# One change to an attention kernel on one core: value products in pieces of two blocks, value scaling on GpSimd, own weight buffers for ScalarE, a new start, planner constants tuned anew

## The chip, the cores and the metric

The kernel runs on one core of one Trainium2 chip. The metric is the device time of one execution in microseconds (us), as the median of several executions. The profile is one execution; its span is some 1.9 us shorter than the device time.

PE is the matrix engine, ACT is ScalarE, DVE is VectorE, POOL is GpSimd. SP issues most of the DMAs.

## The reference, cut to what matters

```python
# q: (8, 1024, 16, 64), k and v: (8, 1024, 64); all 16 heads share k and v
scores = np.matmul(q, k.transpose(0, 1, 3, 2)) / np.sqrt(head_dim)
weights = np.exp(scores - np.max(scores, axis=-1, keepdims=True))
weights = weights / np.sum(weights, axis=-1, keepdims=True)
attn_out = np.matmul(weights, v)
```

The exponentials are the bulk: 8 x 16 x 1024 x 1024 of them. The kernel skips the maximum and gets the row sums from a column of ones beside the values.

## The kernel before

The work is cut into 64 pairs of heads, and each pair into 8 weight tiles (128 keys x 2 heads x 1024 queries), 512 tiles in all. PE makes a tile's scores in two halves ("qk"), each half in one of three PSUM slots. A tile then takes one of two ways. On ACT, two ACTIVATEs of 128x1024 do the exponential. On DVE, two evictions ("z") turn the scores into 16-bit patterns, and four more steps make three factors of them (here `wt`, `z` and `m`), each of which is multiplied with its own copy of the values, scaled by a constant. PE adds up the value products ("av") in one of two accumulators, for three groups of 6, 4 and 6 blocks of 128 queries. DVE divides the result by its sums ("rec", "norm").

A planner in Python runs once, when the kernel is built. It simulates the engines with the constants below and fixes the order of instructions on PE, ACT and DVE. So an engine that is late makes the ones behind it wait (in e6 PE stands 1.13 us for one late DVE factor).

```python
ACT_P, ACT_L = 0.905, 1.19
LAST, SPLIT = 14, 4          # the last 14 tiles all go to ACT
WBUFS = 25
ZBUFS = 6
TERMS = (1.0, 1.017578125, 0.66650390625)
BLOCKS = (0, 6, 10, 16)
# ... in plan(): a group is entered once all 8 tiles of its pair are known
                parts = [
                    (j, k) for j in range(NKT) for k in range(len(TERMS))
                    if k == 0 or NKT * p + j in vtiles
                ] if nt >= NKT * (p + 1) else None
# ...
            cost = AV_B * size[pick[0][1]] if pick else 0.0
# ... in the kernel:
    def scale_v(b):
        st = kst[b]
        st["v"] = vals[b % 2]
        for x, c in zip(st["v"], TERMS):
            nc.vector.tensor_scalar(
                out=x[:, :, 0:D], in0=st["vn"], scalar1=c, scalar2=None, op0=ALU.mult)
# ...
    def exp_act(t, c):
        nc.scalar.activation(
            out=wt[t][:, :, c * QC : (c + 1) * QC], in_=sc.pop((t, c)), func=EXP, scale=ascale
        )
# ...
    def value(p, grp, j, k, n, end, s):
        # ...
        for x in range(BLOCKS[grp], BLOCKS[grp + 1]):    # all 4 or 6 blocks of the group
            # ... one 128x128 weight load and one product of 65 columns for each block
```

Both kinds of tile take their weight buffer from one pool of 25 (`wt`), so an ACTIVATE may have to wait for the earlier user of its buffer on DVE or on ACT itself, in addition to PE. The start transposes all keys and queries of the first pair before the first score.

The softmax here doesn't subtract the row's maximum and nothing guards it: scores larger than these inputs give would overflow.

## Time and profile before

| | before |
|---|---|
| device time, median | 766.85 us (4 runs before the prediction), 766.3 us with the later ones (13 runs) |
| first ACTIVATE starts, last one ends | 8.2 us, 759.4 us |
| ACTIVATEs | 814, 0.904 us apart when nothing hinders (median of the start times) |
| lost between ACTIVATEs | 14.7 us: the sum over all of them of the distance of starts less 0.904 us |
| tail after the last ACTIVATE | 6.4 us |

Three lines from the head of the page and its group lines; after the bar come busy us and mean ns of one instruction, then idle us before them.

```profile
span 765.8 us, 29940 instructions
PE 739.3 (97%) x13616; PEld 486.6 (64%) x13616; DVE 721.0 (94%) x1043; ACT 750.4 (98%) x817; POOL 45.7 (6%) x61
...
L411 ACT ACTIVATE wt<-sc 128x1024 f16<-128x1024 f32 x814 | 748.0, 1241 | 3.8 <-PE sc L401 3.4
...
L434 DVE TENSOR_SCALAR wt<-z 128x2048 uint16<-128x2048 uint16 x105 | 71.2, 678 | 0.2
...
L319 DVE TENSOR_SCALAR vals<-vn 128x512 f16<-128x512 f32 x24 | 9.1, 432 | 0.0
```

ACT is busy for nearly the whole span. So the time is the number of ACTIVATEs times their distance, plus what comes before the first and after the last. PE's 97% says less, since matmul spans overlap: the page has 8192 value products of 194 ns each in the mean, but busy for only 377 us together. The mean of 1241 ns is not the cost of one ACTIVATE either: 814 of them would make 1010 us, and the page has them busy for 748. Successive ones overlap, and the distance of their starts (0.904 us) is what counts.

The front, from the timeline of ACT (start us, length us, what, idle before it and what ended that):

```profile
8.23 13.86 ACT L411 ACTIVATE wt<-sc 128x1024 f16<-128x1024 f32 x15 [0.67 <-PE sc L401]
22.75 1.02 ACT L411 ACTIVATE wt<-sc 128x1024 f16<-128x1024 f32 x1 [0.66 <-PE sc L401]
24.17 2.92 ACT L411 ACTIVATE wt<-sc 128x1024 f16<-128x1024 f32 x3 [0.39 <-PE sc L401]
27.79 2.91 ACT L411 ACTIVATE wt<-sc 128x1024 f16<-128x1024 f32 x3 [0.70 <-PE sc L401]
```

The stream begins at 8.23 us and breaks several times between 22 and 28 us. The timeline of DVE over the same stretch:

```profile
12.27 0.69 DVE L434 TENSOR_SCALAR wt<-z 128x2048 uint16<-128x2048 uint16 x1
12.88 0.69 DVE L437 TENSOR_SCALAR u<-z 128x2048 uint16<-128x2048 uint16 x1
...
14.74 1.22 DVE L423 TENSOR_SCALAR z<-sc 128x1024 uint16<-128x1024 f32 x1
...
18.87 1.45 DVE L319 TENSOR_SCALAR vals<-vn 128x512 f16<-128x512 f32 x3
20.24 0.68 DVE L437 TENSOR_SCALAR u<-z 128x2048 uint16<-128x2048 uint16 x1
20.84 1.21 DVE L423 TENSOR_SCALAR z<-sc 128x1024 uint16<-128x1024 f32 x1
```

The three scalings of the values stand at 18.87 us in DVE's order, ahead of the eviction at 20.84 us, whose PSUM slot PE needs for the next scores. PE's timeline has the wait (1.19 us, until an eviction "z" was done):

```profile
22.11 1.03 PE L401 MATMUL sc<-qt,k2t 64*128 64x512 f16 x4 [1.19 <-DVE z L423]
```

The end, from the timeline of all engines:

```profile
756.05 3.32 ACT L411 ACTIVATE wt<-sc 128x1024 f16<-128x1024 f32 x3
...
757.60 4.14 PE L454 MATMUL acc<-vals,wt 128*128 128x65 f16 x128
...
762.01 0.56 DVE L476 TENSOR_TENSOR osb<-acc,rec 128x384 f32<-128x384 f32 x1
```

PE has 128 value products left after its last score. ACT ends at 759.37 us (756.05 + 3.32), and PE 2.4 us after it.

Busy us of the engines in the middle (PE, PEld, DVE, ACT, POOL; then clock, DMA share, GB/s):

```profile
100.00:600.00 500.00, 491.87 (x9170) 326.04 (x9169) 485.86 (x702) 499.10 (x545) 32.39 (x34) 1.00 0.58 102
```

DVE is at 97.2% there (485.86 of 500).

### The profile page before, as it was taken

What the parts mean: (1) busy time and instruction counts of PE and PEld (TensorE: products, weight loads), DVE (VectorE), ACT (ScalarE), POOL (GpSimd) and SP (SyncE); (2) the same over time, 40 slices, a digit from 0 to 9 for tenths busy, and PEclk for the clock granted to TensorE, in tenths of its full rate; (3) what the DMA queues carried; (4) which work ended last, traced back from release to release, by engine and by line L of the source; (5) the groups of instructions that cost most, each with busy time, mean ns of one, the idle gap of its engine ahead of it and who ended that gap; (6) DMA issues with size and microseconds to landing.
All of it is one profiled execution on the core that took longest, in us unless ns stands there. A gap on an engine that the chain in (4) does not pass through costs nothing.

```text
span 765.8 us, 29940 instructions
## 1 busy us (share of the span) xinstructions
PE 739.3 (97%) x13616; PEld 486.6 (64%) x13616; DVE 721.0 (94%) x1043; ACT 750.4 (98%) x817; POOL 45.7 (6%) x61
## 2 busy tenths in 40 slices
PE   6998999999999999999999999999999999999997
PEld 2565666666666666666666666666666666666676
DVE  5999999999999999899999999999999999999982
ACT  6999999999999999999999999999999999999996
POOL 2100010000100001000010000100001000000000
PEclk9999999999999999999999999999999999999999
DMA  7955675355754447644584644756529455532323
GB/s 110 137 96 103 106 105 110 73 105 105 112 109 89 95 88 109 115 100 83 95 130 84 111 102 82 112 112 99 108 65 132 89 94 102 97 72 58 85 57 85
DMA packets 189839, 75.06 MB, mean 98 GB/s; under 512 B 90256, under 2 KB 188560, under 8 KB 189712
## 3 DMA queue, kind: packets, MB, share of 16 engines
q1 hardware_dynamic: 140544, 54.14, 32.0%
q0 software_dynamic: 47840, 18.35, 21.7%
q8 instruction: 106, 1.74, 0.9%
q10 hardware_dynamic: 1328, 0.66, 0.3%
q14 instruction: 21, 0.17, 0.1%
HBM read 39.58 MB, written 33.55 MB: 96 GB/s over the span
## 4 chain that ended last, share of the span: by engine, by line
ACT 39%; PE 35%; DVE 20%; issue 5%; DMA 0%; POOL 0%; DVEq 0%; ACTq 0%
ACT wt L411 39%; PE acc L454 20%; PE sc L401 14%; DVE z L423 7%; DVE m L441 3%; DVE m L440 3%; DVE osb L476 2%; DVE u L437 2%; DVE wt L434 1%; DVE vals L319 1%; DVE rec L467 1%; DMA kn<-in_k_dram 0%; PE qps L394 0%; POOL k L369 0%; PE kps L389 0%
## 5 line engine op out<-in xcount | busy, mean ns | idle before, releaser
L411 ACT ACTIVATE wt<-sc 128x1024 f16<-128x1024 f32 x814 | 748.0, 1241 | 3.8 <-PE sc L401 3.4
L454 PE MATMUL acc<-vals,wt 128*128 128x65 f16 x8192 | 377.2, 194 | 2.5 <-issue 1.7
L401 PE MATMUL sc<-qt,k2t 64*128 64x512 f16 x2048 | 356.8, 388 | 14.5 <-ACT wt L411 6.4
L454 PEld LDWEIGHTS <-wt 128*128 128x128 f16 x8192 | 295.4, 97 | 116.6 <-issue 116.1
L423 DVE TENSOR_SCALAR z<-sc 128x1024 uint16<-128x1024 f32 x210 | 256.1, 1220 | 21.2 <-PE sc L401 16.6
L401 PEld LDWEIGHTS <-k2t 64*128 64x128 f16 x2048 | 100.6, 93 | 100.1 <-issue 55.4
L440 DVE TENSOR_TENSOR m<-u 128x2048 f16<-128x2048 f16 x105 | 126.4, 1204 | 0.2
L441 DVE TENSOR_TENSOR m<-z,m 128x2048 f16<-128x2048 f16 x105 | 126.3, 1203 | 0.0
L454 PE MATMUL acc<-vals,z 128*128 128x65 f16 x1680 | 103.2, 194 | 0.0
L476 DVE TENSOR_TENSOR osb<-acc,rec 128x384 f32<-128x384 f32 (+1 forms) x192 | 96.6, 503 | 0.4
L454 PE MATMUL acc<-vals,m 128*128 128x65 f16 x1680 | 94.4, 194 | 0.0
L454 PEld LDWEIGHTS <-m 128*128 128x128 f16 x1680 | 67.1, 97 | 32.1 <-issue 32.1
L454 PEld LDWEIGHTS <-z 128*128 128x128 f16 x1680 | 71.0, 97 | 20.2 <-issue 20.2
L434 DVE TENSOR_SCALAR wt<-z 128x2048 uint16<-128x2048 uint16 x105 | 71.2, 678 | 0.2
L437 DVE TENSOR_SCALAR u<-z 128x2048 uint16<-128x2048 uint16 x105 | 70.9, 675 | 0.0
L343 POOL DMA_DIRECT2D qn<-in_q_dram x32 | 29.6, 926 | 616.6 <-DMA qt<-qn 615.2
L467 DVE RECIPROCAL rec<-acc 128x6 f32<-128x6 f32 (+1 forms) x192 | 34.8, 181 | 13.7 <-PE acc L454 13.7
L304 POOL DMA_DIRECT2D k<-in_k_dram x14 | 13.8, 991 | 0.0
L319 DVE TENSOR_SCALAR vals<-vn 128x512 f16<-128x512 f32 x24 | 9.1, 432 | 0.0
L389 PE MATMUL kps<-ident,k 128*128 128x128 f16 x8 | 1.2, 305 | 5.3 <-POOL k L369 5.1
L391 ACT COPY k2t<-kps 128x512 f16<-128x512 f16 x2 | 1.2, 586 | 3.3 <-PE kps L389 3.3
L385 DVE CAST k<-kn 128x512 f16<-128x512 f32 x1 | 0.4, 426 | 4.1 <-DMA kn<-in_k_dram 4.1
(16 smaller groups left out, 8.6 us busy)
## 6 DMA issues: line engine op xcount, KB each, us to landing
out_dram<-osb SPq DMA_DIRECT2D x63, 512.0 KB, 3.7
qn<-in_q_dram POOLq DMA_DIRECT2D x31, 512.0 KB, 7.9
vn<-in_v_dram SPq DMA_DIRECT2D x8, 256.0 KB, 3.1
k<-in_k_dram POOLq DMA_DIRECT2D x14, 128.0 KB, 7.2
qf<-in_q_dram ACTq DMA_DIRECT2D x2, 256.0 KB, 4.3
qt<-qn SPq DMA_TRANSPOSE x32, 4.8
out_dram<-osb SPq DMA_DIRECT2D x2, 192.0 KB, 2.6
kn<-in_k_dram SPq DMA_DIRECT2D x1, 256.0 KB, 3.4
```

The lines of the kernel that those rows point to most:

```text
L319: nc.vector.tensor_scalar(out=x[:, :, 0:D], in0=st["vn"], scalar1=c, scalar2=None, op0=ALU.mult)
L343: nc.gpsimd.dma_start(out=qn[ps[0]].rearrange("p (c r) x -> p c (r x)", r=len(ps)), in_=q[b, :, 2 * hp : 2 * hp + 2 * len(ps), :].rearrang ...
L401: nc.tensor.matmul(sc[t, c][:, h, :], kst[p // HP]["k2t"][64 * h : 64 * h + 64, j, :], qt[p][64 * h : 64 * h + 64, 4 * c : 4 * c + 4, :], ...
L411: nc.scalar.activation(out=wt[t][:, :, c * QC : (c + 1) * QC], in_=sc.pop((t, c)), func=EXP, scale=ascale)
L423: nc.vector.tensor_scalar(out=z[:, :, c * QC : (c + 1) * QC], in0=sc.pop((t, c)), scalar1=vscale, scalar2=(15 + math.log2(C0)) * ONE, op0= ...
L434: lambda: V.tensor_scalar(out=wt[t].bitcast(U16), in0=z, scalar1=0xFC00, scalar2=None, op0=ALU.bitwise_and),
L437: lambda: V.tensor_scalar(out=u, in0=z, scalar1=1023, scalar2=14 << 10, op0=ALU.bitwise_and, op1=ALU.bitwise_or),
L440: lambda: V.tensor_tensor(out=m, in0=h, in1=h, op=ALU.mult),
L441: lambda: V.tensor_tensor(out=m, in0=z.bitcast(FP16), in1=m, op=ALU.mult),
L454: nc.tensor.matmul(acc[p, grp][:, o : o + D + 1], w[:, h, i * P : (i + 1) * P], kst[p // HP]["v"][k][:, j, 0 : D + 1], start=(n == 0 and o ...
L467: nc.vector.reciprocal(out=rec[p, grp][:, 0 : a.shape[1]], in_=a[:, :, D])
L476: nc.vector.tensor_tensor(out=o.rearrange("p i (h d) -> p (i h) d", h=2)[:, BLOCKS[grp] : BLOCKS[grp + 1], :], in0=a[:, :, 0:D], in1=rec.p ...
```

## The change

Its intent is to have fewer ACTIVATEs, fewer waits between them, and shorter ends. It has five parts.

1. Value products are given out in pieces of two blocks (`STEP = 2`) instead of whole groups, and a group takes up tiles as they become known.
2. The scaling of the values moves from DVE to GpSimd. That of batch 0 also comes earlier, right after the first two entries of the plan.
3. ACT's tiles get 26 weight buffers of their own. DVE's tiles write their first factor into a separate buffer `e`. A declaration tells the framework that ACT need not wait for its own earlier write to the same buffer.
4. The start is cut in two: 28 warm-up products on an identity run before the first transposes, the first scores come after half of the transposes, and four filler products follow each early score.
5. The planner's constants are tuned anew. With them it gives 107 tiles to DVE (105 before), so there are 810 ACTIVATEs (814 before).

```diff
-ACT_P, ACT_L = 0.905, 1.19
+ACT_P, ACT_L = 0.9167, 1.19
-MARGIN, WAIT = 0.29, 0.18
-END, END_LAG = 4.84, 0.175
+MARGIN, WAIT = 0.3178, 0.1145
+END, END_LAG = 3.962, -0.318
-BACKLOG, BACK_END = 5.67, 4.09
-LAST, SPLIT = 14, 4
-WBUFS = 25
-ZBUFS = 6
+BACKLOG, BACK_END = 5.253, 2.836
+LAST, SPLIT = 10, 4
+WBUFS = 26
+ZBUFS = 5
+STEP = 2
 ... (planner: pieces of STEP blocks, tiles as they become known)
-            cost = AV_B * size[pick[0][1]] if pick else 0.0
+            cost = AV_B * STEP
 ...
-    osbp = ctx.enter_context(tc.tile_pool(name="osbp", bufs=3))
+    osbp = ctx.enter_context(tc.tile_pool(name="osbp", bufs=2))
 ...
-            nc.vector.tensor_scalar(
+            nc.gpsimd.tensor_scalar(
                 out=x[:, :, 0:D], in0=st["vn"], scalar1=c, scalar2=None, op0=ALU.mult)
 ... (turn_first: one half per call)
+        old = writers.pop((wt[t].name, c), None)
+        if old is not None:
+            tc.declare_no_dep(ins, old, reason="the value products between wait for it")
+        writers[wt[t].name, c] = ins
 ...
+        wt[t] = dvp.tile([P, 2, S], FP16, tag="e", bufs=ZBUFS, name=f"e{name}")
 ...
-        turn_first()
-        load_q(2)
+        warm = psp.tile([P, 2, QC], FP32, tag="sc2", name="warm")
+        for i in range(28):
+            nc.tensor.matmul(
+                warm[:, 0, 0:P], ident, ident, start=True, stop=True, skip_group_check=True)
+        turn_first(0)
         trans_q(1)
-        for _, _, (op, *args) in plan(NP, NKT)[0]:
+        for n, (_, _, (op, *args)) in enumerate(order):
+            if n == 2:
+                turn_first(1)
+                load_q(2)
+                scale_v(0)
+                fill = psp.tile([P, QC], FP32, tag="acc1", name="fill")
 ...
                 score(*args)
+                for i in range(4 if n > 2 and not acc else 0):
+                    nc.tensor.matmul(
+                        fill[:, 0:P], ident, ident, start=True, stop=True, skip_group_check=True)
```

More of the change, by code (lines that the diff above doesn't have):

```diff
@@ L30 @@
 VEC_DEP = 0.12
-BACKLOG, BACK_END = 5.67, 4.09
-LAST, SPLIT = 14, 4
-WBUFS = 25
-ZBUFS = 6
-LAG = 1.37
+BACKLOG, BACK_END = 5.253, 2.836
+LAST, SPLIT = 10, 4
+WBUFS = 26
+ZBUFS = 5
+LAG = 1.362
 FAR = 1e9
 BLOCKS = (0, 6, 10, 16)
+STEP = 2
 def follows(x, y):
@@ L73, in plan @@
     vring: list = []
+    aring: list = []
     ready: dict = {}
@@ L86, in plan @@
             T = pe
-            b = len(ring)
             rest = (2 * NT - nq) / (2 * NKT)
-            if not units and nt < NT and (b < WBUFS or used[ring[b - WBUFS]] > 2.9):
+            if not units and nt < NT and (
+                len(aring) < WBUFS or used[aring[-WBUFS]] > 2.9
+            ):
                 todo = (
@@ L104, in plan @@
                     nt += 1
+                aring += range(nt, nt + 1 if nt < NT - SPLIT else NT)
                 if nt < NT - SPLIT:
@@ L120, in plan @@
                 a = 0 if all(x[3] for x in groups) else 1
-                parts = [
-                    (j, k) for j in range(NKT) for k in range(len(TERMS))
-                    if k == 0 or NKT * p + j in vtiles
-                ] if nt >= NKT * (p + 1) else None
-                if parts is None:
-                    break
-                groups.append((p, g, parts, a, len(parts)))
+                groups.append([p, g, [], a, 0, 0])
                 g = (g + 1) % 3
@@ L131, in plan @@
             for grp in groups:
-                gp, gg, left, a, parts = grp
-                for j, k in left:
+                gp, gg, left, a, n, known = grp
+                for t in ring[NKT * gp + known : NKT * (gp + 1)]:
+                    left += [
+                        (t - NKT * gp, k, x) for k in range(len(TERMS) if t in vtiles else 1)
+                        for x in range(BLOCKS[gg], BLOCKS[gg + 1], STEP)
+                    ]
+                    grp[5] += 1
+                for j, k, x in left:
                     t = NKT * gp + j
@@ L138, in plan @@
                         r = max(ready.get((t, c), FAR) for c in ((0,), (0, 1), (1,))[gg])
-                    if len(left) == parts:
+                    if n == 0:
                         r = max(r, acc[a])
                     if r < tav and (tav > T or grp is groups[0]):
-                        tav, pick = r, (grp, (j, k))
+                        tav, pick = r, (grp, (j, k, x))
             rest = (2 * NT - nq) / (2 * NKT)
             lag = min(LAG, END_LAG + (LAG - END_LAG) * rest / END)
-            cost = AV_B * size[pick[0][1]] if pick else 0.0
+            cost = AV_B * STEP
             av = tav <= T + (SWITCH if mode != "av" else 0) and (
@@ L184, in plan @@
                 pe, mode = st + cost + (AV_1 if mode == "qk" else 0), "av"
-                grp, (j, k) = pick
-                gp, gg, left, a, parts = grp
+                grp, (j, k, x) = pick
+                gp, gg, left, a, n, known = grp
                 t = NKT * gp + j
-                emit(st, "av", gp, gg, j, k, parts - len(left), len(left) == 1, a)
-                left.remove((j, k))
-                share = 1 / len(TERMS) if t in vtiles else 1.0
+                left.remove((j, k, x))
+                end = known == NKT and not left
+                emit(st, "av", gp, gg, j, k, x, n, end, a)
+                grp[4] += 1
+                share = STEP / size[gg] / (len(TERMS) if t in vtiles else 1)
                 nv += share
                 used[t] += share
-                if not left:
+                if end:
                     acc[a] = FAR
@@ L268 @@
     kvp = ctx.enter_context(tc.tile_pool(name="kvp", bufs=2))
-    qp = ctx.enter_context(tc.tile_pool(name="qp", bufs=2))
     qtp = ctx.enter_context(tc.tile_pool(name="qtp", bufs=2))
-    wtp = ctx.enter_context(tc.tile_pool(name="wtp", bufs=WBUFS))
     dvp = ctx.enter_context(tc.tile_pool(name="dvp", bufs=2))
     recp = ctx.enter_context(tc.tile_pool(name="recp", bufs=4))
-    osbp = ctx.enter_context(tc.tile_pool(name="osbp", bufs=3))
+    osbp = ctx.enter_context(tc.tile_pool(name="osbp", bufs=2))
     psp = ctx.enter_context(tc.tile_pool(name="psp", bufs=1, space=bass.MemoryType.PSUM))
@@ L285 @@
             nc.gpsimd.memset(y[:, :, D : D + 2], c)
+    wbuf = [consts.tile([P, 2, S], FP16, name=f"w{i}") for i in range(WBUFS)]
+    order, vtiles = plan(NP, NKT)
+    qbuf = [consts.tile([P, 2 * NKT, P], FP16, name=f"qn{i}") for i in range(2)]
+    writers: dict = {}
     kst: dict = {}
@@ L341, in load_q @@
         if p not in qn:
-            qn[p] = queries(qp, "qn", p, 0)
+            qn[p] = qbuf[p // 2 % 2 ^ 1][:, 0 : NKT * len(ps), :]
         nc.gpsimd.dma_start(
@@ L370, in load_first @@
         st["kn"] = kn
-        qn[0] = queries(qp, "qn", 0, 0)
-        qn[1] = queries(qp, "qn", 1, 0)
+        qn[0], qn[1] = (x[:, 0:NKT, :] for x in qbuf)
         st["vn"] = kvp.tile([P, NKT, D], FP32, tag="vn", bufs=1, name="vn0")
@@ L376, in load_first, with turn_first @@
         qt[0] = queries(qtp, "qt", 0, 1)
-    def turn_first():
+    def turn_first(c):
         st = kst[0]
-        k16 = st["k16"]
-        kps = psp.tile([P, NKT, P], FP16, tag="acc0", name="kps")
-        qps = psp.tile([P, NKT, P], FP16, tag="acc1", name="qps")
-        st["k2t"] = kvp.tile([P, NKT + 1, P], FP16, tag="k2t", name="k2t0")[:, 0:NKT, :]
-        nc.vector.tensor_copy(out=k16[:, :, 0, :], in_=st["kn"])
-        for c in range(NQC):
-            x = slice(4 * c, 4 * c + 4)
-            for i in range(4 * c, 4 * c + 4):
-                nc.tensor.transpose(
-                    kps[:, i, :], k16[:, i, :, :].rearrange("p r d -> p (r d)"), ident)
-            nc.scalar.copy(out=st["k2t"][:, x, :], in_=kps[:, x, :])
-            nc.vector.tensor_copy(out=qn[0][:, x, :], in_=st["qf"][:, x, :])
-            for i in range(4 * c, 4 * c + 4):
-                nc.tensor.transpose(qps[:, i, :], qn[0][:, i, :], ident)
-            nc.vector.tensor_copy(out=qt[0][:, x, :], in_=qps[:, x, :])
+        x = slice(4 * c, 4 * c + 4)
+        if c == 0:
+            st["k2t"] = kvp.tile([P, NKT + 1, P], FP16, tag="k2t", name="k2t0")[:, 0:NKT, :]
+            st["kps"] = psp.tile([P, NKT, P], FP16, tag="acc0", name="kps")
+            st["qps"] = psp.tile([P, NKT, P], FP16, tag="acc1", name="qps")
+            nc.vector.tensor_copy(out=st["k16"][:, :, 0, :], in_=st["kn"])
+        ks, qs = [
+            [
+                lambda i=i: nc.tensor.transpose(st["kps"][:, i, :], st["k16"][
+                    :, i, :, :].rearrange("p r d -> p (r d)"), ident)
+                for i in range(4 * c, 4 * c + 4)
+            ],
+            [
+                lambda i=i: nc.tensor.transpose(st["qps"][:, i, :], qn[0][:, i, :], ident)
+                for i in range(4 * c, 4 * c + 4)
+            ],
+        ]
+        nc.vector.tensor_copy(out=qn[0][:, x, :], in_=st["qf"][:, x, :])
+        for f in ks + qs if c == 0 else qs + ks:
+            f()
+        if c == 0:
+            nc.scalar.copy(out=st["k2t"][:, x, :], in_=st["kps"][:, x, :])
+        nc.vector.tensor_copy(out=qt[0][:, x, :], in_=st["qps"][:, x, :])
+        if c == 1:
+            nc.vector.tensor_copy(out=st["k2t"][:, x, :], in_=st["kps"][:, x, :])
     def score(t, c, s):
@@ L406, in score @@
             )
-        if t not in wt:
-            wt[t] = wtp.tile([P, 2, S], FP16, tag="wt", name=f"wt{t}")
+        if t not in wt and t not in vtiles:
+            wbuf.append(wbuf.pop(0))
+            wt[t] = wbuf[-1]
     def exp_act(t, c):
-        nc.scalar.activation(
-            out=wt[t][:, :, c * QC : (c + 1) * QC], in_=sc.pop((t, c)), func=EXP, scale=ascale
-        )
+        w = wt[t][:, :, c * QC : (c + 1) * QC]
+        ins = nc.scalar.activation(out=w, in_=sc.pop((t, c)), func=EXP, scale=ascale).ins
+        old = writers.pop((wt[t].name, c), None)
+        if old is not None:
+            tc.declare_no_dep(ins, old, reason="the value products between wait for it")
+        writers[wt[t].name, c] = ins
     def exp_dve(t, c):
@@ L429, in exp_dve @@
         V = nc.vector
-        u = dvp.tile([P, 2, S], U16, tag="u", name=f"u{name}")
         m = ms[t] = dvp.tile([P, 2, S], FP16, tag="m", bufs=ZBUFS, name=f"m{name}")
-        h = u.bitcast(FP16)
+        wt[t] = dvp.tile([P, 2, S], FP16, tag="e", bufs=ZBUFS, name=f"e{name}")
         steps[t] = (
@@ L437, in exp_dve, with value @@
             lambda: V.tensor_scalar(
-                out=u, in0=z, scalar1=1023, scalar2=14 << 10,
+                out=m.bitcast(U16), in0=z, scalar1=1023, scalar2=14 << 10,
                 op0=ALU.bitwise_and, op1=ALU.bitwise_or),
-            lambda: V.tensor_tensor(out=m, in0=h, in1=h, op=ALU.mult),
+            lambda: V.tensor_tensor(out=m, in0=m, in1=m, op=ALU.mult),
             lambda: V.tensor_tensor(out=m, in0=z.bitcast(FP16), in1=m, op=ALU.mult),
         )
-    def value(p, grp, j, k, n, end, s):
+    def value(p, grp, j, k, x, n, end, s):
         if n == 0:
@@ L450, in value @@
         w = (wt[t], zs[t].bitcast(FP16), ms[t])[k] if t in zs else wt[t]
-        for x in range(BLOCKS[grp], BLOCKS[grp + 1]):
-            i, h = divmod(x, 2)
-            o = (x - BLOCKS[grp]) * (D + 1)
+        for y in range(x, x + STEP):
+            i, h = divmod(y, 2)
+            o = (y - BLOCKS[grp]) * (D + 1)
             nc.tensor.matmul(
@@ L456, in value @@
                 kst[p // HP]["v"][k][:, j, 0 : D + 1],
-                start=(n == 0 and o == 0), stop=end, skip_group_check=True,
+                start=(n == 0 and y == x), stop=end, skip_group_check=True,
             )
@@ L502, in begin @@
                 trans_q(w + 2)
-        if w == 1:
-            scale_v(0)
         b, hp = divmod(w, HP)
@@ L518 @@
     with tc.manual_schedule(engines={ENG.PE, ENG.Activation, ENG.DVE, ENG.Pool}):
-        turn_first()
-        load_q(2)
-        trans_q(1)
-        for _, _, (op, *args) in plan(NP, NKT)[0]:
+        warm = psp.tile([P, 2, QC], FP32, tag="sc2", name="warm")
[3 more added lines that the diff above has]
+        turn_first(0)
+        trans_q(1)
+        for n, (_, _, (op, *args)) in enumerate(order):
[4 more added lines that the diff above has]
+                fill = psp.tile([P, QC], FP32, tag="acc1", name="fill")
             if op == "qk":
-                while begun <= args[0] // NKT:
+                while n > 2 and begun <= args[0] // NKT:
                     begin(begun)
```

## The prediction

> **What bounds the kernel.** ScalarE's exponentials. The page has ACT busy 750.4 of 765.8 us (98%), PE 97%, DVE 94%. The timeline has the first ACTIVATE at 8.2 us and the last one's end at 759.4 us, 814 of them back to back. By the instructions' start times an unhindered ACTIVATE follows the last after 0.904 us (median); the mean distance is 0.922. So 814 x 0.904 = 736 us is work and 14.7 us is lost between ACTIVATEs: 9.6 us in 56 waits over 0.04 us, 5 us in slips under that. Of the 9.6 us, about 2.4 lie at 20 to 28 us, where PE is still cold (64x512 score pairs about 0.42 us apart; 0.22 later) and DVE does the value scaling; about 3.2 follow the seven later value scalings (three DVE operations of 0.43 us each, in VectorE's order ahead of a score eviction); 1.8 are two single waits near 323 and 673 us; the rest are slips of 0.06 us. Before the stream come 8.2 us of loads and transposes, after it 6.4 us: 2.4 us of PE backlog (128 value products after the last score), reciprocal and normalise 0.8, store 3.
>
> **What the change does, and what it is worth.**
> 1. Two more weight tiles go to VectorE (107 for 105): 810 ACTIVATEs, 4 x 0.904 = -3.6 us. VectorE pays 2 x 5.8 us and hands 9.1 us of value scaling to GpSimd; it stays near 97-98% full in the middle.
> 2. Head: scores start after half of the transposes, and 28 warm-up products heat PE. I estimate the first ACTIVATE near 6.7 us, but the second waits for the other half of the queries, near 8.1 (9.15 now): net -1.1 us. Warm PE and no scaling on VectorE at 19-27 us: -1.7 us.
> 3. Scaling on GpSimd: it no longer delays evictions, but 24 GpSimd operations near 0.9 us each (the cast of this size took 0.87 us)[...] So only -1.5 of the 3.2 us.
> 4. ACT alone owns its weight buffers and the write-after-write wait is declared away: 387 ACTIVATEs now have a second wait (17 ns semaphore instructions); the compiled order has single waits. Such ACTIVATEs average only some 3 ns more: -1.2 us.
> 5. Value products go out in pieces of two blocks, for tiles already there: fewer late scores, -0.9 us. The 64 added products and the fillers fall on PE slack.
> 6. Tail: 60 value products after the last score instead of 128, most of them ready: -1.6 us, though two normalises now come together.
>
> Nearly all of this is on the critical path, since each term shortens the ACT stream or its ends. Sum -11.6 us; I take 754.5 us, a little less optimistic than the sum once slips are counted against ACT's faster supply. The range is 750.5 to 760. Faster by over 2% (below 751.5) 0.18, within 2% 0.80, slower 0.02.
>
> **What would show it.** ACTIVATE x810; first near 6.7 us; mean distance 0.911 to 0.918; no second-wait instructions on ACT; no wait clusters after value scaling; the last ACTIVATE's end to the span's end near 4.8 us; sc pairs at 0.22 us from the start.
>
> **What would make it wrong.** VectorE, nearly full, becomes the limiter (longer z waits, ACT waiting on PE that waits on DVE for PSUM); GpSimd scaling stretches VectorE's two-input multiplications; finer pieces cost PE more than 0.03 us a product or switch more often; the warm-up delays the first transposes; PE cools again. On the good side, the slips vanish altogether and ACT runs at 0.905.

The sum is that of its six steps, -3.6 - 2.8 - 1.5 - 1.2 - 0.9 - 1.6 = -11.6 us.

"Cold" and "warm" in it are what the traces show of PE's clock. Before, the clock record has no entry until it begins, with the full clock, at 27.4 us, and a pair of score products takes 0.61 us at 23.5 us and 0.39 at 28.3 us. In the changed kernel, with the warm-up products, it begins at 4.6 us. PE "cools again" in e1 (half clock from 12.2 to 19.1 us) and in e9 (from 744.1 to 747.6 us). The stretch of the two-input multiplications is in the trace of the changed kernel: of the 13 that run beside a GpSimd scaling, four take 1.50 to 1.63 us and nine 1.18 to 1.26; away from the scalings none takes over 1.23 us.

## The result, and the profile after

The changed kernel takes 759.65 us (median of 9 runs, 758.79 to 761.25) against 766.3 us (13 runs). The ratio is 0.9913, with a 95% interval of 0.9903 to 0.9922. Ratios here are the mean time of one kernel's fast runs over that of the other's of the same rounds, so they are not quite the ratio of the medians. The gain is 6.65 us, where 12.35 had been foretold. By its stated range (750.5 to 760) the forecast was right, at the very edge of the range; its sizes were not.

The page after, the same lines (here `w` is what `wt` was for ACT, and `e` for DVE):

```profile
span 757.1 us, 29891 instructions
PE 729.6 (96%) x13784; PEld 490.3 (65%) x13784; DVE 727.7 (96%) x1032; ACT 745.9 (99%) x812; POOL 87.0 (11%) x85
...
L431 ACT ACTIVATE w<-sc 128x1024 f16<-128x1024 f32 x810 | 744.0, 1254 | 2.3 <-PE sc L419 1.8
...
L455 DVE TENSOR_SCALAR e<-z 128x2048 uint16<-128x2048 uint16 x107 | 74.6, 698 | 0.2
...
L328 POOL TENSOR_SCALAR vals<-vn 128x512 f16<-128x512 f32 x24 | 42.1, 1761 | 1.2
```

There are 810 ACTIVATEs as foretold. A scaling takes 1.76 us on GpSimd, where I had estimated 0.9. DVE's 16-bit step is 20 ns longer in the mean.

The front of ACT after:

```profile
6.61 1.02 ACT L431 ACTIVATE w<-sc 128x1024 f16<-128x1024 f32 x1 [0.74 <-PE sc L419]
8.06 8.64 ACT L431 ACTIVATE w<-sc 128x1024 f16<-128x1024 f32 x9 [0.43 <-PE sc L419]
17.11 7.81 ACT L431 ACTIVATE w<-sc 128x1024 f16<-128x1024 f32 x8 [0.40 <-PE sc L419]
25.13 5.63 ACT L431 ACTIVATE w<-sc 128x1024 f16<-128x1024 f32 x6 [0.21 <-PE sc L419]
```

The first ACTIVATE is 1.6 us earlier, but there are breaks at 7, 17 and 25 us. DVE after, and GpSimd beside it:

```profile
11.44 1.13 DVE L455 TENSOR_SCALAR e<-z 128x2048 uint16<-128x2048 uint16 x1
12.49 1.08 DVE L458 TENSOR_SCALAR m<-z 128x2048 uint16<-128x2048 uint16 x1
...
14.76 1.22 DVE L445 TENSOR_SCALAR z<-sc 128x1024 uint16<-128x1024 f32 x1
```

```profile
8.38 4.65 POOL L328 TENSOR_SCALAR vals<-vn 128x512 f16<-128x512 f32 x3
```

The two 16-bit steps at 11.44 and 12.49 us take 1.13 and 1.08 us, not 0.69, while GpSimd scales from 8.38 to 13.03 us. The third eviction starts at 14.76 us, at the same time as before (14.74), though ACT had begun 1.6 us earlier.

The end, and the middle:

```profile
747.02 5.13 ACT L431 ACTIVATE w<-sc 128x1024 f16<-128x1024 f32 x5
...
750.45 2.17 PE L475 MATMUL acc<-vals,w 128*128 128x65 f16 x60
...
753.25 0.56 DVE L497 TENSOR_TENSOR osb<-acc,rec 128x384 f32<-128x384 f32 x1
```

```profile
100.00:600.00 500.00, 487.77 (x9272) 326.77 (x9270) 496.35 (x702) 499.75 (x546) 63.00 (x52) 1.00 0.58 103
```

ACT ends at 752.15 us and PE 0.5 us after it. In the middle DVE has gone from 97.2% to 99.3%, while ACT gets through 546 ACTIVATEs in 500 us instead of 545. So ACT's pace in the middle has hardly changed.

The start times of the ACTIVATEs give the whole account. I took a second profile of the kernel before in run e12. "Lost" is the distance from one start to another, less 0.904 us for each ACTIVATE between.

| us | before | before again (e12) | after | after less mean of the two |
|---|---|---|---|---|
| first ACTIVATE | 8.23 | 8.19 | 6.61 | -1.6 |
| lost from 1st to 31st | 2.46 | 1.70 | 2.35 | +0.3 |
| the ACTIVATEs themselves | 814 x 0.904 | 814 x 0.904 | 810 x 0.904 | -3.6 |
| lost from 31st to the last one's start | 12.21 | 11.51 | 10.40 | -1.5 |
| tail | 6.42 | 6.55 | 4.91 | -1.6 |
| span | 765.8 | 764.4 | 757.1 | -8.0 |

The rows above the span add up to some 0.6 us less than it, because the last ACTIVATE is counted at 0.904 us and takes 1.45 to 1.52. The profiled run after is 0.7 us faster than its median, and the first of the two before is 1.3 us slower than its own, the second as fast as it. That takes 0.7 and half of 1.3 off the 8.0 and leaves the 6.65 us of the medians.

### The profile page after: what moved, and what is told of

Read it like the earlier page. It is cut to its first block, busy times and chain, and to the rows that moved or that the text cites. A ratio compares the mean times of both kernels' runs of the same rounds, so it can differ in the third digit from the quotient of the medians.

```text
span 757.1 us, 29891 instructions
## 1 busy us (share of the span) xinstructions
PE 729.6 (96%) x13784; PEld 490.3 (65%) x13784; DVE 727.7 (96%) x1032; ACT 745.9 (99%) x812; POOL 87.0 (11%) x85
## 4 chain that ended last, share of the span: by engine, by line
ACT 84%; DVE 8%; PE 7%; issue 1%; DMA 0%; POOL 0%
ACT w L431 84%; PE acc L475 4%; DVE z L445 3%; PE sc L419 3%; DVE m L462 1%; DVE m L461 1%; DVE e L455 1%; DVE m L458 1%; DVE osb L497 1%; DMA kn<-in_k_dram 0%; DVE rec L488 0%; POOL k L378 0%; PE qps L402 0%; DVE qt L411 0%; DVE k2t L413 0%
## 5 line engine op out<-in xcount | busy, mean ns | idle before, releaser
L431 ACT ACTIVATE w<-sc 128x1024 f16<-128x1024 f32 x810 | 744.0, 1254 | 2.3 <-PE sc L419 1.8
L419 PE MATMUL sc<-qt,k2t 64*128 64x512 f16 x2048 | 341.0, 382 | 20.1 <-ACT w L431 9.4
L475 PE MATMUL acc<-vals,w 128*128 128x65 f16 x6480 | 325.6, 193 | 0.7 <-DVE osb L497 0.3
L475 PEld LDWEIGHTS <-w 128*128 128x128 f16 x6480 | 246.7, 97 | 92.6 <-issue 91.7
L419 PEld LDWEIGHTS <-k2t 64*128 64x128 f16 x2048 | 97.2, 93 | 87.8 <-issue 39.0
L461 DVE TENSOR_TENSOR m<-m 128x2048 f16<-128x2048 f16 x107 | 129.8, 1214 | 0.5
L475 PE MATMUL acc<-vals,e 128*128 128x65 f16 x1712 | 121.7, 194 | 0.3 <-DVE osb L497 0.2
L475 PEld LDWEIGHTS <-e 128*128 128x128 f16 x1712 | 79.2, 97 | 27.9 <-issue 27.8
L455 DVE TENSOR_SCALAR e<-z 128x2048 uint16<-128x2048 uint16 x107 | 74.6, 698 | 0.2
L458 DVE TENSOR_SCALAR m<-z 128x2048 uint16<-128x2048 uint16 x107 | 73.8, 690 | 0.0
L328 POOL TENSOR_SCALAR vals<-vn 128x512 f16<-128x512 f32 x24 | 42.1, 1761 | 1.2
```

The costliest lines, as they stand in the source:

```text
L328: nc.gpsimd.tensor_scalar(out=x[:, :, 0:D], in0=st["vn"], scalar1=c, scalar2=None, op0=ALU.mult)
L419: nc.tensor.matmul(sc[t, c][:, h, :], kst[p // HP]["k2t"][64 * h : 64 * h + 64, j, :], qt[p][64 * h : 64 * h + 64, 4 * c : 4 * c + 4, :], ...
L431: ins = nc.scalar.activation(out=w, in_=sc.pop((t, c)), func=EXP, scale=ascale).ins
L455: lambda: V.tensor_scalar(out=wt[t].bitcast(U16), in0=z, scalar1=0xFC00, scalar2=None, op0=ALU.bitwise_and),
L458: lambda: V.tensor_scalar(out=m.bitcast(U16), in0=z, scalar1=1023, scalar2=14 << 10, op0=ALU.bitwise_and, op1=ALU.bitwise_or),
L461: lambda: V.tensor_tensor(out=m, in0=m, in1=m, op=ALU.mult),
```

## The experiments

Each was timed on the same chip as runs of the kernel before, and "ratio" is always to that kernel; the changed kernel's is 0.9913. A hundredth of ratio is 7.7 us. The first four shared a chip, and so did the next four and the last four.

| run | what | median us | ratio, 95% interval |
|---|---|---|---|
| e1 | changed, scaling on DVE | 764.02 | 0.9972 (0.9959 to 0.9985) |
| e2 | changed, no scaling from batch 2 on | 763.25 | 0.995 (0.9928 to 0.9972) |
| e3 | changed, old start | 759.83 | 0.9919 (0.9906 to 0.9932) |
| e4 | changed, second waits back | 759.29 | 0.9914 (0.9901 to 0.9927) |
| e5 | changed, tiny scaling from batch 2 on | 759.08 | 0.9913 (0.99 to 0.9926) |
| e6 | changed, batches 1 to 7 scaled on DVE | 762.35 | 0.9956 (0.9943 to 0.9969) |
| e7 | changed, whole groups | 765.46 | 0.9995 (0.9983 to 1.0007) |
| e8 | before, scaling on GpSimd | 765.09 | 0.999 (0.9977 to 1.0002) |
| e9 | changed, 104 DVE tiles, fewer at the end | 766.36 | 0.9998 (0.9986 to 1.001) |
| e10 | changed, 104 DVE tiles, fewer throughout | 763.9 | 0.9976 (0.9964 to 0.9988) |
| e11 | changed, first scaling later | 764.56 | 0.9974 (0.996 to 0.9988) |
| e12 | before, once more | 766.5 | 1.0004 (0.9987 to 1.0022) |

### e3: the old start

The edit restores `turn_first()` as it was and takes away the warm-up products and the fillers. The scaling stays on GpSimd.

```diff
-        (28 warm-up products)
-        turn_first(0)
-        trans_q(1)
+        turn_first()
+        load_q(2)
+        trans_q(1)
+        scale_v(0)
...
-            if n == 2:
-                turn_first(1)
-                ...
-                for i in range(4 if n > 2 and not acc else 0):
-                    (filler product)
```

> The changed kernel with the old start: all transposes before the first score, no warm-up products, no fillers; the scaling stays on GpSimd. The prediction's step 2 put the new head at 1.1 us before the second ACTIVATE and 1.7 us in the front: 762.4. A reading of the two traces (slips before 30 us 2.4 us before, 1.7 us after without the late second ACTIVATE) says 1.1 + 0.7: 761.4. First ACTIVATE near 8.2 us, second near 9.15, score pairs 0.42 us apart until about 25 us.

Measured: 759.83 us, ratio 0.9919. The new start is worth 0.5 us by the ratios, which the intervals do not tell from nothing. The prediction had 2.8 us, and so both readings of the expectation were too high. ACT's front in this run:

```profile
7.84 15.93 ACT L421 ACTIVATE w<-sc 128x1024 f16<-128x1024 f32 x17 [0.59 <-PE sc L409]
23.94 6.79 ACT L421 ACTIVATE w<-sc 128x1024 f16<-128x1024 f32 x7 [0.17 <-PE sc L409]
```

With the old start ACT begins at 7.84 us and runs almost without a break. In the changed kernel it begins at 6.61 us and breaks. The 31st ACTIVATE starts at 36.05 us here and at 36.08 us in the changed kernel. The clock record of the trace gives PE its full clock only from 24.6 us on here, against 4.6 us in the changed kernel (a score pair took 0.61 us at 22.08 us here, and 0.39 us at 25.56 us), and still nothing is lost. So with the old start neither ACT's start nor PE's clock paces the front. The new start is more open to the clock: in e5, e9 and e10, which have it too, the clock record gives full clock only from 10.3 to 10.6 us on, the second ACTIVATE starts at 9.12 to 9.15 us and the 31st at 36.5 us, some 0.4 us later than in the changed kernel. In both runs DVE does its third eviction at about the same time, 14.89 us here and 14.76 us in the changed kernel, and the order has the ACTIVATEs wait for PSUM slots that DVE holds. The line here is:

```profile
14.89 1.22 DVE L435 TENSOR_SCALAR z<-sc 128x1024 uint16<-128x1024 f32 x1
```

I call DVE's chain the likely pacer; that is read from the timelines, and e11 bears it out only in part.

### e1 and e6: the scaling back on DVE

```diff
-            nc.gpsimd.tensor_scalar(
+            nc.vector.tensor_scalar(                        # e1
+            (nc.vector if b else nc.gpsimd).tensor_scalar(  # e6
```

> The changed kernel with the value scaling put back on VectorE, nothing else. The trace of the changed kernel shows the 24 GpSimd scalings at 1.75 us each (I had estimated 0.9) and VectorE's 16-bit steps beside them at 1.1 us in place of 0.69. Theory A[...]: within 0.8 us of the changed kernel's 759.65, and the 16-bit steps are back at 0.68 us. Theory B (the move itself is a gain, as the prediction's step 3 had it): 1.5 us slower, 761.2. If GpSimd's scaling is a loss: 758.5 or less.

Theory A is that GpSimd's scaling costs the kernel about as much as the scaling on VectorE did.

Measured: 764.02 us, 4.4 us slower than the changed kernel, more than any theory had said. The front alone lost 2.3 us more than the changed kernel's (4.63 us up to the 31st ACTIVATE against 2.35). The timeline shows how:

```profile
8.19 1.10 DVE L328 TENSOR_SCALAR vals<-vn 128x512 f16<-128x512 f32 x3 [0.18 <-DMA vn<-in_v_dram]
...
10.48 0.39 PE L419 MATMUL sc<-qt,k2t 64*128 64x512 f16 x2 [1.81 <-DVE z L445]
...
13.93 0.61 PE L419 MATMUL sc<-qt,k2t 64*128 64x512 f16 x2
```

The scaling came ahead of the first eviction, PE stood still for 1.81 us waiting for it, and from 12.2 to 19.1 us the granted clock was one half (score pairs of 0.61 instead of 0.39 us). The fall came 1.7 us after the end of the gap of 1.81 us; what set it off is not shown. As e1 mixes two effects, e6 keeps the front as changed.

> The changed kernel with batch 0 scaled on GpSimd and batches 1 to 7 on VectorE. Run e1 had all eight on VectorE and was 4.4 us slower, but its first scaling came ahead of the first eviction, PE ran idle and the clock fell to half for 6.8 us. Here the front is the changed kernel's. Theory F (the new plan leaves VectorE so little room that 7 x 1.25 us of its time now cost more than the 3.2 us that they cost in the kernel before): 3 to 4.5 us slower than 759.65, 763 to 764. Rival (e1 was slow for its front alone): 760.5 or less.

Measured: 762.35 us, ratio 0.9956, so 2.7 us slower by the medians and 3.3 by the ratios. Theory F foretold 3 to 4.5, so it holds in kind. The slips of ACT of over 0.04 us, from the start of each of the seven DVE scalings to six us after its end, add up to 5.9 us here and to 3.2 us in the kernel before, for the same work on DVE. After the first of them, in PE's timeline:

```profile
65.30 0.22 PE L475 MATMUL acc<-vals,z 128*128 128x65 f16 x2
66.65 0.35 PE L475 MATMUL acc<-vals,m 128*128 128x65 f16 x6 [1.13 <-DVE m L462]
```

PE, whose order is fixed, waits 1.13 us for a DVE factor that the scaling delayed, and ACT loses 1.26 us. By these sums an insertion of 1.25 us on DVE costs 0.84 us in the mean here and 0.46 in the kernel before. I read it as the new order leaving DVE less room; no run tests that by itself.

### e8: the kernel before with only the scaling moved

```diff
-            nc.vector.tensor_scalar(
+            nc.gpsimd.tensor_scalar(
```

> The kernel before with nothing but its value scaling moved to GpSimd. Theory: the move is worth the front's 1.7 us and at most the 3.2 us of slips after the seven later scalings, less what GpSimd's hold costs: 762 to 764 against 766. Rival (the move alone is worth little, the gain is the plan's): 765 or more. Also a second look at the two waits of 0.9 us near 323 and 673 us in the profile of before: if they are that one run's, they are not here.

"GpSimd's hold" is what the trace of the changed kernel shows: DVE's 16-bit steps took 1.13 and 1.08 us in place of 0.69 while GpSimd was scaling.

Measured: 765.09 us, ratio 0.999, which may be nothing and is at most 0.23%. The rival holds: the move alone is worth little. Its trace does show the foretold effect, since the front up to the 31st ACTIVATE loses 0.96 us (2.46 and 1.70 in the two profiles before) and the slips within six us of the seven later scalings fall from 3.2 to 1.9 us. But the small slips under 0.04 us grew from 5.0 to 6.1 us, and three pauses of PE took 2.7 us of ACT (see e12). So the scaling pays in the new plan (e6) and hardly in the old one.

### e2 and e5: hardly any scaling

```diff
-        for x, c in zip(st["v"], TERMS):
+        for x, c in zip(st["v"], TERMS) if b < 2 else ():     # e2
...
-                out=x[:, :, 0:D], in0=st["vn"], ...
+                (two columns only, for batches 2 to 7)           # e5
```

Both give wrong results.

> The changed kernel with the value scaling left out for batches 2 to 7 (wrong result on purpose: they use the values of batch 0 or 1). This is the most that any place for the scaling could give. Theory A (contention eats the gain): 757.5 or less, with no waits of ACT of over 0.1 us in the half-dozen us after the places where the scaling stood. Rival C (the remaining slips come from the fixed order on PE and from PSUM slots, not from the scaling): 759 or more, and the sum of slips between ACTIVATEs over 0.04 us stays near 8 us.

Measured: four runs between 762.9 and 764.3 us, two at 758.6 and 759.2. It tells nothing of the scaling. With no reader of the values left, the framework put five value loads ahead of the first output store in SP's queue, and one normalise on DVE waited for an output buffer:

```profile
59.80 0.56 DVE L497 TENSOR_TENSOR osb<-acc,rec 128x384 f32<-128x384 f32 x1 [3.71 <-DMA out_dram<-osb]
```

> The changed kernel with the scalings of batches 2 to 7 cut to two columns (wrong result on purpose). Run e2 had left them out, and with their readers gone the DMA queue put five value loads ahead of the first output store, so that one normalise waited 3.7 us for an output buffer; here the compiled order of that queue is the changed kernel's own. Theory A (the GpSimd scalings still cost, through VectorE): the 1.9 us of slips in the six us after them vanish, 758 or less. Rival C (the slips are the fixed order's own): 759.3 to 760.

Measured: 759.08 us, ratio 0.9913, the changed kernel's own. Rival C holds by the clock: what scaling is left on GpSimd costs no time that these runs can tell. The slips after the six small scalings did fall, from 1.7 to 0.35 us, but the small slips rose from 4.4 to 5.3 us.

### e4: the second waits

```diff
-        if old is not None:
+        if False:
             tc.declare_no_dep(ins, old, reason="the value products between wait for it")
```

> The changed kernel without the declaration that ACT's writes to one buffer need no wait: 755 of 810 ACTIVATEs get a second wait (387 of 814 had one in the kernel before). Theory D (each second wait costs the 3 ns that I read from the trace of before): 2.3 us slower, 762. Rival E (the wait is for an ACTIVATE 26 tiles ago, its 17 ns lie in the shadow of the running ACTIVATE): within 0.8 us of 759.65. The small slips under 0.04 us, 4.4 us in sum in the changed kernel, tell which.

The trace has the second waits, by the view of the ACTIVATE's source line:

```profile
L431 ACTq EVENT_SEMAPHORE  x755: 17/17/17, 55.4 to 750.7; - x189
```

Measured: 759.29 us, ratio 0.9914. Rival E holds: 755 extra waits of 17 ns cost nothing that these runs can tell. The difference of 3 ns that I had read between ACTIVATEs with and without a second wait in the kernel before was no cost of the wait.

### e7: whole groups

```diff
-STEP = 2
+STEP = 6, 4, 6          # and STEP[group] where STEP stood
```

> The changed kernel with value products given out by whole groups (6, 4 and 6 blocks) as before, in place of pieces of two; all else as changed. The planner then finds 105 VectorE tiles and 814 ACTIVATEs. Prediction's steps 1, 5 and 6 (3.6 us for four ACTIVATEs, 0.9 for fewer late scores, part of 1.6 of the tail): 764 to 765. If the pieces matter for the tile count alone: 763.3. If they do nothing: 760.

Measured: 765.46 us, ratio 0.9995: without the pieces nothing is left of the gain, although all else is as changed. It splits into two terms. The planner finds 105 DVE tiles, hence four more ACTIVATEs, 3.6 us; and the tail is 7.4 us instead of 4.9. The end of this run:

```profile
755.55 4.51 PE L475 MATMUL acc<-vals,w 128*128 128x65 f16 x140
...
760.33 0.56 DVE L497 TENSOR_TENSOR osb<-acc,rec 128x384 f32<-128x384 f32 x1
```

Counted in PE's order, 176 products come after the last score (the line shows the last 140 of them), where the pieces left 60 and the kernel before 128. In the middle the pieces are worth little: from the 31st ACTIVATE on this run loses 10.8 us, the changed kernel 10.4.

The run leaves a rival: it keeps constants that were tuned for the pieces, and its tail is 1 us longer than that of the kernel before. No run has the pieces with the old constants. But the planner is plain Python in the kernel files, and run without the chip it gives the counts, though no times: 105 DVE tiles and 128 late products for the kernel before, 105 and 176 for this run, 107 and 60 for the changed kernel, as in the traces. With the pieces and all of the old constants it gives 106 and 244, and with `ACT_P` alone of the new ones 106 and 64. So the pieces by themselves are not enough: the second tile and the short tail need the new constants too.

### e9 and e10: fewer tiles on DVE

```diff
-LAST, SPLIT = 10, 4
+LAST, SPLIT = 24, 4                  # e9
-BACKLOG, BACK_END = 5.253, 2.836
+BACKLOG, BACK_END = 3.5, 2.836       # e10
```

> The changed kernel with VectorE kept from the last 24 weight tiles in place of the last 10: 104 VectorE tiles and 816 ACTIVATEs, the first 480 tiles planned as in the changed kernel. If the tile count is worth what the prediction's step 1 said, six more ACTIVATEs cost 6 x 0.904 = 5.4 us: 765.1. Rival (at the end other engines bind, tiles there are free): 761 or less.

Measured: 766.36 us, 6.7 more than the changed kernel. Six ACTIVATEs are 5.4 us, and its trace has one new wait of 1.2 us at 746 us. There PE's clock was at half, from 744.1 to 747.6 us by the clock record, and a score pair took 0.61 us instead of 0.39:

```profile
743.89 0.40 PE L419 MATMUL sc<-qt,k2t 64*128 64x512 f16 x2 [0.24 <-ACT w L431]
744.80 0.61 PE L419 MATMUL sc<-qt,k2t 64*128 64x512 f16 x2 [0.18 <-ACT w L431]
745.35 2.27 PE L475 MATMUL acc<-vals,w 128*128 128x65 f16 x38
```

What set off the fall is not shown. Tiles at the end are not free.

> The changed kernel with a smaller limit on VectorE's backlog: also 104 VectorE tiles and 816 ACTIVATEs, but the three tiles are missing from all over the middle (14 14 13 13 13 13 14 10 per batch against 15 13 14 13 14 14 13 11). If VectorE's fullness makes the middle's slips (those between 30 and 730 us, 6.0 us over 0.04 us each in the changed kernel), this is 1.5 us or more faster than run e9, and the slips there fall under 4 us. Rival (slips are the fixed order's, whatever VectorE's load): within 0.8 us of run e9.

Measured: 763.9 us, 2.5 us less than e9. But the reason was not the one expected. DVE's share of the middle falls back to 97.4%, and the slips of ACT between 30 and 730 us stay at 5.4 us (5.9 in e9, 6.0 in the changed kernel):

```profile
100.00:600.00 500.00, 483.35 (x9100) 323.60 (x9096) 486.75 (x685) 500.00 (x547) 59.74 (x51) 1.00 0.56 102
```

So DVE's fullness as such does not make the slips of the middle, and that theory falls. Of the 2.5 us, 1.2 are e9's wait at the end. The two profiles differ by no more than 1.3 us, as the profiled run of e10 was 1.2 us slower than its median, so the rest is not in the traces. By the ratios the six ACTIVATEs cost 4.8 us here, which confirms the price of the tile count to within the noise.

### e11: the first scaling later

```diff
                 load_q(2)
-                scale_v(0)
...
+            if w == 0:
+                scale_v(0)      # after load_q(4)
```

> An attempt at a faster front: the changed kernel with batch 0's GpSimd scaling put behind the next query load, so that it runs near 19 to 23.5 us instead of 8.4 to 13 us, when VectorE's first 16-bit steps took 1.13 and 1.08 us in place of 0.69. If VectorE's chain paces the front, the third eviction comes 0.8 us earlier and the kernel gains up to 0.8 us: 758.9. If the hold only moves to later steps: 759.65, or worse if the first value products have to wait for the values.

```profile
11.69 0.69 DVE L455 TENSOR_SCALAR e<-z 128x2048 uint16<-128x2048 uint16 x1
12.30 0.69 DVE L458 TENSOR_SCALAR m<-z 128x2048 uint16<-128x2048 uint16 x1
...
14.17 1.22 DVE L445 TENSOR_SCALAR z<-sc 128x1024 uint16<-128x1024 f32 x1
```

With GpSimd quiet the two 16-bit steps take 0.69 us again, and the third eviction comes 0.6 us earlier. ACT got 0.2 us of that: its 13th ACTIVATE starts at 18.74 us (18.93 in the changed kernel). This settles that GpSimd's scaling had stretched them, to 1.13 and 1.08 us. It did not stop them: in the changed kernel the DVE step from 11.44 to 12.57 us lay inside the third GpSimd scaling (11.41 to 13.03 us) and did not wait for its end. The spans on GpSimd are rough, so this is a measurement and no proof, and what the two engines contend for is not shown. Yet the run takes 764.56 us. The front up to the 31st ACTIVATE lost 3.0 us (2.35 in the changed kernel). The scaling now held up DVE's steps at 19 to 24 us (a multiplication at 21.64 us took 1.51 us in place of 1.21), with a slip of 0.6 us of ACT at 23 us, and one of 1.2 us followed at 29 us, where PE waited for transposed queries:

```profile
31.01 0.60 PE L419 MATMUL sc<-qt,k2t 64*128 64x512 f16 x4 [1.32 <-DMA qt<-qn]
```

This too comes from the moved scaling. In SP's queue the query transposition stands behind the next load of values, and that load waited 12.9 us for the scaling, which reads the same buffer: the scaling ended at 24.53 us, the load was issued at 24.55 and the transposition at 25.00 us (13.03, 13.06 and 17.75 us in the changed kernel). And at 58 us ACT lost 4.3 us in one piece, because a normalise waited 3.5 us for an output buffer, as in e2; from 60.5 to 67.3 us PE was then at half clock, and ACT lost another 1.1 us. The change has cut the output buffers from three to two. Two of ten variants of the changed kernel ran into this wait; the changed kernel itself did not. Whether three buffers would cure it was not tried.

### e12: the kernel before again

> The kernel before once more, for a second profile. Its first profile has two pauses of PE of 1 us near 324 and 674 us, inside runs of value products and without any semaphore; run e8, the same plan, had three at other times (183, 322, 463), and no profile of the plan with pieces of two has any. If they belong to the old order of instructions, one or more is here, at about the same place in the order; if they are chance, there may be none. Time 765 to 767.

Measured: 766.5 us. There are again two pauses of PE without a semaphore, of 0.7 and 0.9 us, but at 114 and 184 us. In the first profile, PE's timeline shows one inside a run of value products:

```profile
323.09 0.44 PE L454 MATMUL acc<-vals,wt 128*128 128x65 f16 x9
324.41 0.25 PE L454 MATMUL acc<-vals,wt 128*128 128x65 f16 x3 [0.88 <-issue]
```

I counted products in PE's order. The pauses of over 0.5 us in the middle, two each in the two profiles of before, three in e8 and one in e7, start at product numbers 1630, 2910, 2910, 5469, 5469, 8029, 11868 and 6877. All of these leave 92 to 94 when divided by 128. A product is two instructions (a weight load and a matmul), so every pause stands at the same place in a period of 256 instructions, also in e7, where 104 warm-up and filler products stand ahead. The page before has a DMA queue of the kind "instruction" (q8) with 106 packets; by the DMA records each has 16384 bytes, and they come 7.0 us apart in the median. PE's 27232 matmuls and weight loads are 257 for each of these packets. Before each of the pauses the packet came 10.6 to 12.0 us after the one before it. I read it as PE running out of instructions; that is an inference, and no run put it to the test. Why a packet is late is open, and not every late one makes a pause (11.2 us in e4 and e5 without). No profile of the changed order with pieces of two had such a pause in the middle, outside the stretches at half clock. The pauses cost ACT 1.8 and 1.3 us in the two profiles before. This is part of the 1.5 us gained there, seen and not tested.

No version beats the changed kernel clearly. Runs e3, e4 and e5 equal it within their intervals (e5 with a wrong result).

## Why the prediction was right or wrong

The range held, barely, and the class (within 2%) was right. That the range held is luck as much as insight: three of the nine runs lie above its 760 us, and the gain was half of the point estimate. Term by term:

| step of the prediction | foretold us | the runs |
|---|---|---|
| 1, four ACTIVATEs fewer | -3.6 | -3.6 by count; e9 and e10 bear out the price |
| 2, head and front | -2.8 | -1.3 at the 31st ACTIVATE; the new start gives none of it (e3) |
| 3, scaling on GpSimd, batches 1 to 7 | -1.5 | slips of over 0.04 us after it from 3.2 and 3.1 to 2.0, so 1.1 to 1.3 less |
| 4, second waits | -1.2 | 0 (e4) |
| 5, fewer late scores | -0.9 | steps 3 to 5 together -1.5 |
| 6, tail | -1.6 | -1.6; it needs the pieces (e7), with the new constants |
| sum | -11.6 | -8.0 between profiles, -6.65 between medians |

**Step 2 failed.** The prediction said "net -1.1 us" for the earlier second ACTIVATE and "Warm PE and no scaling on VectorE at 19-27 us: -1.7 us". ACT did start at 6.61 us as foretold, and the second ACTIVATE at 8.06, also as foretold. But I counted an earlier start as a gain without asking what the ACTIVATEs after it wait for. By the timelines they wait for slots that DVE holds, and DVE was no earlier, its first steps being stretched by GpSimd. The lead was gone by the 13th ACTIVATE (18.93 us against 19.12 before). The part that is real, about 1.3 us at the 31st, also comes with the old start and a cold PE (31st ACTIVATE at 36.05 us with the full clock from 24.6 us on, against 36.08 with it from 4.6 us on), so against the old start a warm PE was worth nothing there. It came with the scaling's leaving DVE's front: e8, with the old start and only that moved, reaches its 31st ACTIVATE at 35.9 us.

**Step 4 failed.** A mean difference of 3 ns between two kinds of ACTIVATE, in one trace, was taken for a cost. With 755 such waits the kernel took 759.29 us, 0.4 less than with none, so the waits cost nothing that these runs can tell. That they lie in the shadow of the running ACTIVATE is a guess; no run shows where.

**Step 3 was about right in the slips and wrong in the operation's size.** The prediction said "24 GpSimd operations near 0.9 us each", and they took 1.76. GpSimd's scaling did stretch DVE's steps (1.13 us for 0.69, e11), and this cost nothing measurable after the first batches (759.08 us with hardly any scaling, e5, against 759.65). The sentence that DVE "stays near 97-98% full" was wrong: 99.3%.

**Step 5** looked for late scores. What the pieces gave, with the constants tuned for them, was in steps 1 and 6, and without it nothing of the gain is left (e7). Part of the credit went to the two waits of 0.9 us at 323 and 673 us, which were pauses of PE without a semaphore, at places that differ from run to run (e12).

**The sum itself** has a slip: 766.85 - 11.6 is 755.25, and I wrote 754.5 and called it "a little less optimistic", while it is more so. With 755.25 the miss would have been 4.4 us.

What is open: why the slips under 0.04 us between ACTIVATEs (3.9 to 6.1 us in sum) come and go between variants, why an instruction packet is late, what the pieces would be worth in time with the old constants, and what the rest of the difference between e9 and e10 is.

## What to carry to other kernels

Where one engine sets the time with a fixed number of instructions, look first for what lets the planner take an instruction off it, and at how much work the other engines still have when it ends; finer pieces of PE work, with constants tuned for them, gave both, and with whole groups nothing of the gain was left. An earlier start of the busiest engine is worth only what is still there some thirty instructions later, so compare the two traces at that point and not at the first instruction. A wait that the trace shows need not cost anything (here 755 of 17 ns each: 759.29 us, against 759.65 with none): put it in twice as often and time it.
